# One pool of 4 KB tiles and longer leads in a two-layer decoder kernel

## The chip, the cores and the metric

The kernel runs on one core of a Trainium2 chip. The metric is the time of one execution on the device in microseconds; the time given for a kernel is the median of its runs.

## The reference

Two decoder layers on 512 rows of width 1024 in float32, each followed by a SwiGLU feed-forward with a hidden width of 2816. The first mixes by a gated MLP, the second by retention with four heads. Every part starts with an RMS norm, and the result is added to the stream.

```python
h = h + sgu_mixer(rmsnorm(h), ...)      # z = gelu(h @ w_in); u, v halves; u * (W_s LN(v) + b) @ w_out
h = h + swiglu(rmsnorm(h), ...)         # (silu(h @ w_g) * (h @ w_u)) @ w_down
h = h + retention(rmsnorm(h), ...)      # q, k rotated; decayed scores; group norm; * silu(g); @ w_out
h = h + swiglu(rmsnorm(h), ...)
return rmsnorm(h)
```

## The kernel before

All large products are made in float32 precision from three matmuls: each operand is split into a high part (fp32r) and a low part, and `three` adds high x high, high x low and low x high in PSUM. The high part of a weight tile is written by ACT and the low part by VectorE (DVE) in `split`; tiles of weights are 128 x 2 x 512, 4 KB per partition.

Blocks of 1024 x 512 pairs of columns use `seven`, a form of Strassen's product with the seven products P1, P7, P6, Q4, P5, P2, P3 in this order, on quarters of both operands: a gate-up unit (`gu`, five per feed-forward), a down product (`dn`, two per feed-forward, the rest goes through `last_rows`), values and gates of a head (`vg`, four) and half of the output projection of retention (`ro0`). Each of the seven has two jobs, one for each pair of row tiles. Sums of weight quarters come from VectorE, or, for P7 and P5 of `dn`, `vg` and `ro`, from an accumulating load that GpSimd's queue (POOL) issues after the plain load. Sums of the left factor's quarters are made on VectorE by the function `A` and split as well (`h_P7h`, `h_P7l` for instance); `run` asks for the left factors of its own product and of the next two.

The work is a list of jobs, and `pipeline` goes through it: before a job runs, weights are fetched up to six weighted jobs ahead (`FETCH`) and split up to three ahead (`PREP`). A scheduler then sets each engine's order of instructions when the program is built, by the order in which they were written and by when they could run, and tiles are given out of pools in which a new tile waits for an old one to be free. Pool `gen` has 21 tiles of 4 KB, `raws` 8 of 8 KB (rows of hidden values, left factors of the feed-forward and of the heads, copies of the normed input); `XH` and `XL`, the normed input's two parts, have a place of their own. SyncE's queue (SP) issues the plain loads.

The rotary tables (sine and cosine of position angles, some 36 VectorE instructions on 128 x 512) are made in eight steps during the first feed-forward, one after its small first unit (`gl`) and one or two in each unit after it.

Of the kernel before, what the change touches and what calls it, by code (L numbers as in the profile page):

```python
# [25 lines left out]
PREP = 3  # L26
FETCH = 6
N_GEN = 21
N_RAW = 8
N_TMP = 5  # L30
EPS = 1e-6
# [18 lines left out]
class Job:  # L50


    def __init__(self, fetch=None, prep=None, run=None):
        self.fetch, self.prep, self.run = fetch, prep, run


def pipeline(jobs):
    n = len(jobs)
    weighted = [i for i, j in enumerate(jobs) if j.prep is not None]
    f = p = 0  # L60
    done = 0
    for i, job in enumerate(jobs):
        while f < len(weighted) and f < done + FETCH:
            jobs[weighted[f]].fetch()
            f += 1
        while p < len(weighted) and p < done + PREP:
            jobs[weighted[p]].prep()
            p += 1
        if job.prep is not None:
            done += 1  # L70
        job.run()
# [3 lines left out]
def trunk(ctx, tc, x, positions, mix_g, ffn_g, fin_g, sgu_w_in, sgu_w_s, sgu_b_s, sgu_ln_g, sgu_ln_b,  # L75
# [5 lines left out]
    raws = ctx.enter_context(tc.tile_pool(name="raws", bufs=N_RAW))  # L81
# [10 lines left out]
    def RAW(name, dtype=F32, shape=(P, 4, T)):  # L92
        return raws.tile(list(shape), dtype, tag="r", name=name)
# [11 lines left out]

    def captured(*fns):

        n = len(jobs)
        for fn in fns:
            fn()  # L110
        new = jobs[n:]
        del jobs[n:]
        units = []
        for j in new:
            if j.prep is not None or not units:
                units.append([j])
            else:
                units[-1].append(j)
        return units

    def merged(a, b):

        i = j = 0
        while i < len(a) or j < len(b):
            if j == len(b) or (i < len(a) and i * len(b) <= j * len(a)):
                jobs.extend(a[i])
                i += 1
            else:
                jobs.extend(b[j])
                j += 1  # L130
# [82 lines left out]
    XH = xpool.tile([P, KD, T], F32R, name="XH")  # L213
    XL = xpool.tile([P, KD, T], F32R, name="XL")
    X = xpool.tile([P, NC, D], F32, name="X")

    def project_t(name, w, slices, evac, col_of=None, halves=False, mid=None):
# [4 lines left out]
        def run(kp, t0, t1):  # L222
            if not ps:
                ps.extend(PS(f"ps_{name}_{i}") for i in range(2))
            for m in range(4):
                o = ps[m // 2][:, m % 2, t0:t1]
                for a in range(2):
                    k = 2 * kp + a
                    sl = slice(m * P, (m + 1) * P)
                    first = k == 0 and (t1 == T)  # L230
                    three(o, ws[kp].h[:, a, sl], ws[kp].l[:, a, sl], XH[:, k, t0:t1], XL[:, k, t0:t1],
                          first, k == KD - 1)
# [32 lines left out]
    def natural_step(o, c, kp, w):  # L265
        wh, wl = w
        for a in range(2):
            k = 2 * kp + a
            sl = slice(c * P, (c + 1) * P)
            three(o, XH[:, k, sl], XL[:, k, sl], wh[:, a, :], wl[:, a, :], k == 0, k == KD - 1)  # L270
# [3 lines left out]

    def seven(name, w, r0, np_, c1, c2, A, evac, mid=None, dma_sums=False, turned=False):

# [3 lines left out]
        steps = [(s, min(2, np_ - s)) for s in range(0, np_, 2)]  # L280
# [4 lines left out]
        def load(key, i, j, s, nk):  # L285
            raw[key, s] = fetch_tile(f"{name}_{key}_{s}", w, r0 + i * np_ + s, nk, ((c1, T) if j == 0 else (c2, T),))

        def onto(key, i, j, s, nk):
            c0 = c1 if j == 0 else c2
            k0 = r0 + i * np_ + s  # L290
            src = w[k0 * P:(k0 + nk) * P, c0:c0 + T].rearrange("(a p) n -> p a n", p=P)
            nc.gpsimd.dma_start(raw[key, s][:, 0:nk, :], src, accum_op=ALU.add)

        def fetch(p, s, nk):
            if p == "P1":
                load("b11", 0, 0, s, nk)
            elif p == "P7" and dma_sums:
                load("t", 1, 1, s, nk)
                onto("t", 0, 1, s, nk)
            elif p == "P5" and dma_sums:  # L300
                load("b12", 0, 1, s, nk)
                onto("b12", 0, 0, s, nk)
            elif p == "P7":
                load("b12", 0, 1, s, nk)
                load("t", 1, 1, s, nk)
            elif p == "Q4":
                load("b21", 1, 0, s, nk)
            elif p == "P2":
                load("b21", 1, 0, s, nk)
            elif p == "P3":  # L310
                load("b22", 1, 1, s, nk)

        def add(dst, other, s, nk):
            d, o = raw[dst, s][:, 0:nk, :], raw[other, s][:, 0:nk, :]
            nc.vector.tensor_tensor(d, d, o, ALU.add)  # L315

        def prep(p, s, nk):
# [4 lines left out]
            parts[p, s] = split(raw[use, s], f"{name}_{p}_{s}", nk)  # L322

        chain = {"P1": "X", "P7": "Y", "P6": "X", "Q4": "Y", "P5": "X", "P2": "Z", "P3": "X"}
# [3 lines left out]
        def matmuls(p, s, nk, c):  # L328
            o = acc[chain[p]]
            ah, al = A(p)  # L330
            wh, wl = parts[p, s]
            cs = slice(c * P, (c + 1) * P)
            first, last = p in opens, p in closes
            if not turned:
                for a in range(nk):
                    k = s + a
# [790 lines left out]
```

## Time and profile before

| what | us |
|---|---|
| median of 3 runs | 1269.76 |
| lowest, highest run | 1268.45, 1273.49 |
| the profiled execution | 1267.79 |
| its span, first to last instruction | 1266.1 |

| engine | busy us | share |
|---|---|---|
| PE (TensorE matmul) | 1220.4 | 96% |
| PEld (TensorE weight load) | 1081.8 | 85% |
| DVE (VectorE) | 947.4 | 75% |
| ACT (ScalarE) | 616.8 | 49% |
| POOL (GpSimd) | 47.4 | 4% |

The profile names an instruction by its source line, engine, operation and tiles (`out<-in`, with the buffer numbers left out). Matmuls are pipelined and their ends are modelled, so PE idle is what no modelled matmul covers. A granted clock below 1.00 means that TensorE ran slower for a part of the stretch. A wait is put down to the operation that came last; "waited for: us in total, times, longest" stands at the end of such a row.

### The profile page before, as it was taken

What the parts mean: (1) busy time and instruction counts of PE and PEld (TensorE: products, weight loads), DVE (VectorE), ACT (ScalarE), POOL (GpSimd) and SP (SyncE); (2) the same over time, 40 slices, a digit from 0 to 9 for tenths busy, and PEclk for the clock granted to TensorE, in tenths of its full rate; (3) what the DMA queues carried; (4) which work ended last, traced back from release to release, by engine and by line L of the source; (5) the groups of instructions that cost most, each with busy time, mean ns of one, the idle gap of its engine ahead of it and who ended that gap; (6) DMA issues with size and microseconds to landing.
All of it is one profiled execution on the core that took longest, in us unless ns stands there. A gap on an engine that the chain in (4) does not pass through costs nothing. (4 is left out here: it accounts for less than half of the span.)

```text
span 1266.1 us, 18063 instructions
## 1 busy us (share of the span) xinstructions
PE 1220.4 (96%) x7290; PEld 1081.8 (85%) x7290; DVE 947.4 (75%) x1080; ACT 616.8 (49%) x772; POOL 47.4 (4%) x49
## 2 busy tenths in 40 slices
PE   8999999998999999999999999889999999999997
PEld 7787889987999798978878878668899989997995
DVE  4467489999779884786766757697488799878864
ACT  4424255544544463656455564465355445544452
POOL 0000000000001000000000000000000010000000
PEclk9999999999999999999999999899999999999999
DMA  7224225457636763356445645466215476556531
GB/s 266 85 83 128 64 84 156 137 146 228 183 117 164 219 198 94 84 156 169 127 140 125 185 123 150 110 178 211 84 44 174 142 175 196 170 158 187 189 116 67
DMA packets 101987, 183.91 MB, mean 145 GB/s; under 512 B 6376, under 2 KB 19728, under 8 KB 101904
## 3 DMA queue, kind: packets, MB, share of 16 engines
q1 hardware_dynamic: 91984, 163.86, 40.8%
q0 software_dynamic: 9920, 18.90, 9.1%
q8 instruction: 57, 0.93, 0.3%
q14 instruction: 26, 0.21, 0.1%
HBM read 180.64 MB, written 2.10 MB: 144 GB/s over the span
## 5 line engine op out<-in xcount | busy, mean ns | idle before, releaser
L211 PE MATMUL X_gu<-xP_f,wl_gu_P 128*128 128x256 f32 x480 | 135.8, 283 | 0.0
L210 PE MATMUL X_gu<-xP_f,wh_gu_P 128*128 128x256 f32 x480 | 135.8, 283 | 0.0
L209 PE MATMUL X_gu<-xP_f,wh_gu_P 128*128 128x256 f32 x480 | 135.8, 283 | 0.0
L188 DVE TENSOR_TENSOR wl_gu_P<-wr_gu_b,wh_gu_P 128x1024 fp32r<-128x1024 f32 x80 | 95.0, 1219 | 29.6 <-ACT wh_gu_P L187 29.6
L210 PEld LDWEIGHTS X_gu<-xP_f,wh_gu_P 128*128 128x128 f32 x480 | 92.1, 192 | 0.2
L209 PEld LDWEIGHTS X_gu<-xP_f,wh_gu_P 128*128 128x128 f32 x480 | 92.1, 192 | 0.2
L211 PEld LDWEIGHTS X_gu<-xP_f,wl_gu_P 128*128 128x128 f32 x480 | 92.1, 192 | 0.0
L187 ACT ACTIVATE wh_gu_P<-wr_gu_b 128x1024 fp32r<-128x1024 f32 x80 | 79.5, 1052 | 18.4 <-DVE wl_gu_P L188 5.0
L315 DVE TENSOR_TENSOR wr_gu_t<-wr_gu_t,wr_gu_b 128x1024 f32<-128x1024 f32 x60 | 71.7, 1217 | 2.1 <-DMA wr_gu_t<-in_ffn_w_gu 2.0
L187 ACT ACTIVATE wh_gu_P<-wr_gu_t 128x1024 fp32r<-128x1024 f32 x40 | 41.6, 1057 | 50.3 <-DVE wr_gu_t L315 40.6
L188 DVE TENSOR_TENSOR wl_vg_P<-wr_vg_b,wh_vg_P 128x1024 fp32r<-128x1024 f32 x32 | 38.6, 1219 | 26.8 <-ACT wh_vg_P L187 26.8
L209 PE MATMUL ps_qk<-XH,wh_qk 128*128 128x512 f32 (+1 forms) x160 | 56.1, 352 | 1.4 <-ACT xr_r L622 0.8
L211 PE MATMUL ps_qk<-XH,wl_qk 128*128 128x512 f32 (+1 forms) x160 | 55.6, 348 | 0.0
L210 PE MATMUL ps_qk<-XL,wh_qk 128*128 128x512 f32 (+1 forms) x160 | 55.4, 347 | 0.0
L188 DVE TENSOR_TENSOR wl_gu_P<-wr_gu_t,wh_gu_P 128x1024 fp32r<-128x1024 f32 x40 | 48.0, 1218 | 7.1 <-ACT wh_gu_P L187 7.1
L209 PE MATMUL Y_gu<-xP_f,wh_gu_P 128*128 128x256 f32 x160 | 45.3, 283 | 0.0
L210 PE MATMUL Y_gu<-xP_f,wh_gu_P 128*128 128x256 f32 x160 | 45.3, 283 | 0.0
L211 PE MATMUL Y_gu<-xP_f,wl_gu_P 128*128 128x256 f32 x160 | 45.3, 283 | 0.0
L209 PE MATMUL Y_gu<-XH,wh_gu_Q 128*128 128x256 f32 x160 | 45.3, 283 | 0.0
L210 PE MATMUL Y_gu<-XL,wh_gu_Q 128*128 128x256 f32 x160 | 45.3, 283 | 0.0
L211 PE MATMUL Y_gu<-XH,wl_gu_Q 128*128 128x256 f32 x160 | 45.3, 283 | 0.0
L209 PE MATMUL Z_gu<-XH,wh_gu_P 128*128 128x256 f32 x160 | 45.3, 283 | 0.0
(507 smaller groups left out, 3872.9 us busy)
## 6 DMA issues: line engine op xcount, KB each, us to landing
wr_gu_b<-in_ffn_w_gu SPq DMA_DIRECT2D x100, 512.0 KB, 4.0
wr_dn_b<-in_ffn_w_down SPq DMA_DIRECT2D x40, 512.0 KB, 4.6
wr_vg_b<-in_ret_w_in SPq DMA_DIRECT2D x40, 512.0 KB, 3.7
wr_gu_t<-in_ffn_w_gu SPq DMA_DIRECT2D x20, 512.0 KB, 5.2
wr_qk<-in_ret_w_in SPq DMA_DIRECT2D x32, 256.0 KB, 3.1
wr_dn<-in_ffn_w_down SPq DMA_DIRECT2D x12, 512.0 KB, 4.0
wr_ro_b<-in_ret_w_out SPq DMA_DIRECT2D x10, 512.0 KB, 4.1
wr_u<-in_sgu_w_in SPq DMA_DIRECT2D x8, 512.0 KB, 4.1
```

Of the source, the lines that this page charges most:

```text
L187: nc.scalar.activation(h, s, AF.Copy)
L188: nc.vector.tensor_tensor(l, s, f32(h), ALU.subtract)
L209: nc.tensor.matmul(o, ah, bh, start=start, stop=False, skip_group_check=True)
L210: nc.tensor.matmul(o, ah, bl, start=False, stop=False, skip_group_check=True)
L211: nc.tensor.matmul(o, al, bh, start=False, stop=stop, skip_group_check=True)
L315: nc.vector.tensor_tensor(d, d, o, ALU.add)
```

## The change

It has five parts. All 4 KB work goes into one pool `gen` of 38 tiles: 8 KB tiles are cut into a tile for each half of the rows or for each of the high and low parts, and `raws` is gone (`XH` and `XL` get a pool of two tiles). Weights are split five jobs ahead instead of three and fetched eight ahead instead of six, and the accumulating loads with their base loads twelve ahead (`EARLY`). `seven` takes groups of rows (one group in each use here), and in the gate-up units P5 loads both its quarters anew instead of keeping P1's and P7's: 40 more loads of 512 KB. The left factors P1, P7 and P6 of a product are asked for in the block before it, where it was P1 and P7, or P1 alone. The rotary tables' eight steps go to the eight jobs of `u0` and `u1` in the mixing layer.

```diff
-PREP = 3
-FETCH = 6
-N_GEN = 21
-N_RAW = 8
+PREP = 5
+FETCH = 8
+EARLY = 12
+ASK = 3
+N_GEN = 38
+SUMS_X = ("P7", "P5")
+SUMS_GU = ()
...
-    for i, job in enumerate(jobs):
-        while f < len(weighted) and f < done + FETCH:
-            jobs[weighted[f]].fetch()
+    for job in jobs:
+        while e < n and e < done + EARLY:
+            if weighted[e].early:
+                weighted[e].fetch()
+            e += 1
+        while f < n and f < done + FETCH:
+            if not weighted[f].early:
+                weighted[f].fetch()
             f += 1
...
-    raws = ctx.enter_context(tc.tile_pool(name="raws", bufs=N_RAW))
+    xp = ctx.enter_context(tc.tile_pool(name="xp", bufs=2))
...
+            if p == "P7":
+                load("t", 1, 1)
+                (onto if p in dma_sums else load)("t" if p in dma_sums else "o", 0, 1)
...
+            elif p == "P5":
+                load("b12", 0, 1)
+                (onto if p in dma_sums else load)("b12" if p in dma_sums else "o", 0, 0)
...
-            extra = {"P7": "b12", "P6": "b11", "Q4": "b21", "P5": "b11"}.get(p)
-            if extra and not (dma_sums and p in ("P7", "P5")):
-                add(use, extra, s, nk)
+            extra = {"P7": "o", "P6": "b11", "Q4": "b21", "P5": "o"}.get(p)
+            if extra and p not in dma_sums:
...
-                h, l = RAW(f"{name}_h{r}", F32R), RAW(f"{name}_l{r}", F32R)
-                for a in range(0, n, 2):
+                h, l = (G(f"{name}_{q}{r}_{i}", F32R, (P, 4, H))[:, 0:len(ks), :] for q in "hl")
...
+    project_t("u0", w_in, ((0, T),), after_u0, mix0_col, mid={kp: turn_tables for kp in range(4)})
+    project_t("u1", w_in, ((T, T),), after_u1, mix0_col, mid={kp: turn_tables for kp in range(4)})
...
-            nc.vector.tensor_tensor(yraw[j][:, i, :], u, mx[g // 2][:, g % 2, :], ALU.mult)
+            for h in range(2):
+                hs = slice(h * H, (h + 1) * H)
+                nc.vector.tensor_tensor(yq[j][h][:, i, :], u[:, hs], mx[g // 2][:, g % 2, hs], ALU.mult)
...
-        unit(1, {"P5": lambda: A[0]("P1"), "P2": lambda: A[0]("P7")})
+        unit(1, {("Q4", 1): lambda: A[0]("P1", 0), ("P5", 0): lambda: A[0]("P7", 0), ("P2", 1): lambda: A[0]("P6", 0)})
         down(0)
...
-        second({"P2": lambda: outA("P1")} if hd == 3 else None)
+        second({("P6", 1): lambda: outA("P1", 0), ("P2", 0): lambda: outA("P7", 0), ("P2", 1): lambda: outA("P6", 0)} if hd == 3 else None)
```

VectorE's order around the start of the output projection of retention. `vg3` is the last head, `y7_3<-X_vg3` the evacuation of its P5, `s1_3<-Z_vg3` that of its P2, `z...` are left factors, `wl_ro0_...` low parts of the projection's weights, and `X_97<-X_97,X_ro0` adds its first product. Before:

```order
L1016 TENSOR_TENSOR y7_3_6898<-y7_3_6898,X_vg3_6819 128x1024
L992 TENSOR_TENSOR s3_3_7069<-sc3_2_7052,dec3_6809 128x128
L188 TENSOR_TENSOR wl_vg3_P3_0_7076<-wr_vg3_b22_0_6965,wh_vg3_P3_0_7075 128x1024
L995 TENSOR_TENSOR sl3_6990<-s3_3_7069,sh3_6988 128x128
L188 TENSOR_TENSOR wl_vg3_P3_2_7096<-wr_vg3_b22_2_7013,wh_vg3_P3_2_7095 128x1024
L1010 TENSOR_TENSOR s1_3_6850<-s1_3_6850,Z_vg3_7079 128x1024
L1013 TENSOR_TENSOR vl3_0_7113<-s1_3_6850,vh3_0_7112 128x1024
L415 TENSOR_TENSOR z0_P1l_7117<-z0_5564,z0_P1h_7116 128x1024
L188 TENSOR_TENSOR wl_ro0_P1_0_7124<-wr_ro0_b11_0_7031,wh_ro0_P1_0_7123 128x1024
L188 TENSOR_TENSOR wl_ro0_P1_2_7128<-wr_ro0_b11_2_7073,wh_ro0_P1_2_7127 128x1024
L188 TENSOR_TENSOR wl_ro0_P7_0_7159<-wr_ro0_t_0_7092,wh_ro0_P7_0_7158 128x1024
L388 TENSOR_TENSOR z0_S3_7163<-z0_5564 128x1024
```

After:

```order
L1008 TENSOR_TENSOR y7_3_6999<-y7_3_6999,X_vg3_6924 128x1024
L984 TENSOR_TENSOR s3_1_7117<-sc3_0_7100,dec3_6914 128x384
L984 TENSOR_TENSOR s3_2_7165<-sc3_2_7158,dec3_6914 128x256
L170 TENSOR_TENSOR wl_ro0_P1_0_0_7180<-wr_ro0_b11_0_0_7073,wh_ro0_P1_0_0_7179 128x1024
L370 TENSOR_TENSOR z_S3_0_7196<-z0_0_5677,z0_1_5663 128x1024
L987 TENSOR_TENSOR sl3_7098<-s3_1_7117,sh3_7096 128x384
L1002 TENSOR_TENSOR s1_3_6954<-s1_3_6954,Z_vg3_7183 128x1024
L987 TENSOR_TENSOR sl2_3_7099<-s3_2_7165,sh2_3_7097 128x256
L397 TENSOR_TENSOR z_P7l_0_7199<-z_S3_0_7196,z_P7h_0_7198 128x1024
L984 TENSOR_TENSOR s3_3_7175<-sc3_2_7158,dec3_6914 128x128
L170 TENSOR_TENSOR wl_ro0_P1_0_2_7206<-wr_ro0_b11_0_2_7121,wh_ro0_P1_0_2_7205 128x1024
L1005 TENSOR_TENSOR vl3_0_7223<-s1_3_6954,vh3_0_7222 128x1024
```

The first cast of the projection moved ahead of the evacuation `s1_3<-Z_vg3`, and P1's factor (further up) and P7's stand before the projection's first product.

VectorE's order in the first down product of the first feed-forward (`dn0_0`). `quarter_turns` is the last of the rotary tables, `X_97` (after: `X_95`) with `X_dn0_0` is the addition of P1, `wr_dn0_0_t_...` a sum of weights. Before:

```order
L388 TENSOR_TENSOR h0_0_S1_2515<-h0_0_1638,h0_1_2099 128x1024
L840 TENSOR_TENSOR quarter_turns_3458<-quarter_3456,turn19_3459 128x512
L315 TENSOR_TENSOR wr_dn0_0_t_0_2410<-wr_dn0_0_t_0_2410,wr_dn0_0_b11_0_2332 128x1024
L388 TENSOR_TENSOR h0_0_S2_2517<-h0_0_S1_2515,h0_0_1638 128x1024
L415 TENSOR_TENSOR h0_0_P6l_2520<-h0_0_S2_2517,h0_0_P6h_2519 128x1024
L188 TENSOR_TENSOR wl_dn0_0_P7_2_2538<-wr_dn0_0_t_2_2449,wh_dn0_0_P7_2_2537 128x1024
L918 SCALAR_TENSOR_TENSOR h0_1_2099<-X_gu0_1_2043,s1_0_1_2100 128x2x256
L428 TENSOR_TENSOR X_97<-X_97,X_dn0_0_2514 128x2x512
L188 TENSOR_TENSOR wl_dn0_0_P6_0_2558<-wr_dn0_0_t_0_2410,wh_dn0_0_P6_0_2557 128x1024
```

After:

```order
L370 TENSOR_TENSOR h0_0_S2_0_2537<-h0_0_S1_0_2535,h0_0_0_1818 128x1024
L397 TENSOR_TENSOR h0_0_P6l_0_2540<-h0_0_S2_0_2537,h0_0_P6h_0_2539 128x1024
L170 TENSOR_TENSOR wl_dn0_0_P7_0_0_2547<-wr_dn0_0_t_0_0_2302,wh_dn0_0_P7_0_0_2546 128x1024
L410 TENSOR_TENSOR X_95<-X_95,X_dn0_0_2613 128x2x512
L170 TENSOR_TENSOR wl_dn0_0_P7_0_2_2553<-wr_dn0_0_t_0_2_2338,wh_dn0_0_P7_0_2_2552 128x1024
L891 SCALAR_TENSOR_TENSOR h0_1_0_2269<-X_gu0_1_2142,s1_0_1_2200 128x512
L302 TENSOR_TENSOR wr_dn0_0_t_0_0_2302<-wr_dn0_0_t_0_0_2302,wr_dn0_0_b11_0_0_2371 128x1024
L302 TENSOR_TENSOR wr_dn0_0_t_0_2_2338<-wr_dn0_0_t_0_2_2338,wr_dn0_0_b11_0_2_2407 128x1024
L170 TENSOR_TENSOR wl_dn0_0_P6_0_0_2610<-wr_dn0_0_t_0_0_2302,wh_dn0_0_P6_0_0_2609 128x1024
L410 TENSOR_TENSOR X_95<-X_95,Y_dn0_0_2649 128x2x512
```

The rotary row is gone; the addition of P1 moved ahead of P7's second cast, and the sum of weights for P6 that stood ahead of it stands behind it. P6's factor stands ahead of that addition in both.

VectorE's order in the mixing layer, between the statistics of `v` (`mv`, and the steps `ri_ln`, `ry_ln`, `rt_ln` of its inverse root) and its normalization; `wl_u1_...` are casts for the second half of `u`, `sum`, `turn`, `turns` and `frac` rotary steps. Before:

```order
L528 SCALAR_TENSOR_TENSOR ry_ln_0_554<-ru_ln_0_552,ry_ln_548 128x4
L192 SCALAR_TENSOR_TENSOR wl_u1_1_680<-wr_u1_1_509,mix0_cols_108,wh_u1_1_679 128x512
L524 TENSOR_TENSOR rt_ln_1_556<-ry_ln_0_554 128x4
L526 SCALAR_TENSOR_TENSOR ru_ln_1_558<-rt_ln_1_556,ra_ln_544 128x4
L528 SCALAR_TENSOR_TENSOR ry_ln_1_560<-ru_ln_1_558,ry_ln_0_554 128x4
L524 TENSOR_TENSOR rt_ln_2_562<-ry_ln_1_560 128x4
```

After:

```order
L518 SCALAR_TENSOR_TENSOR ry_ln_0_570<-ru_ln_0_568,ry_ln_564 128x4
L734 CAST turn6_728<-sum5_726 128x512
L742 TENSOR_SCALAR turns7_761<-ahl_645 128x512
L514 TENSOR_TENSOR rt_ln_1_572<-ry_ln_0_570 128x4
L735 TENSOR_TENSOR turns_686<-sum5_726,turn6_728 128x512
L734 CAST turn8_764<-turns7_761 128x512
L516 SCALAR_TENSOR_TENSOR ru_ln_1_574<-rt_ln_1_572,ra_ln_560 128x4
L735 TENSOR_TENSOR frac7_763<-turns7_761,turn8_764 128x512
L518 SCALAR_TENSOR_TENSOR ry_ln_1_576<-ru_ln_1_574,ry_ln_0_570 128x4
L757 TENSOR_TENSOR sum8_767<-turns_686,frac7_763 128x512
L514 TENSOR_TENSOR rt_ln_2_578<-ry_ln_1_576 128x4
```

Where single casts stood between the steps of the inverse root, one to three table steps stand now between one and the next; on those steps the normalization of `v` waits.

More of the change, by code (lines that the diff above doesn't have):

```diff
@@ L104, in trunk @@
     jobs = []
[L106 to L130, printed above, removed]
     def then(fn):
@@ L294, in fetch @@
[L294 to L305, printed above, removed]
+            return w[k0 * P:(k0 + nk) * P, c0:c0 + T].rearrange("(a p) n -> p a n", p=P)
@@ L375, in combos @@
-    def combos(name, raw, np_):
+                    matmuls(p, g, s, nk, c)
+            elif n == len(steps) - 1:
+                for c in range(2):
+                    for st_ in steps[-2:]:
+                        matmuls(p, *st_, c)
+                    evac(p, acc, c)
+            if mid and (p, n) in mid:
+                mid[p, n]()
+        for i in range(len(PRODUCTS) * len(steps)):
+            p, st_ = PRODUCTS[i // len(steps)], steps[i % len(steps)]
+            jobs.append(Job(lambda p=p, st_=st_: fetch(p, *st_), lambda p=p, st_=st_: prep(p, *st_), lambda i=i: run(i),
+                            early=p in dma_sums))
@@ L492, in chunk, with start @@
                     step(kp, j, c)
+        def start(kp, j):
+            left(where[2 * kp][0], 1)
+            step(kp, j, 3)
+            left(where[2 * kp][0], 0)
         ends = list(range(n_all, kt // 2))
@@ L874, in feed_forward @@
+    def feed_forward(l, ready):
         w = ffn_w_gu[l]
-        hraw = [None] * 5
-        hlast = []
+        hq = [[None, None] for _ in range(5)]
+        he = []
         xparts = xA(f"f{l}")
-        steps = iter(range(100))
-        def more():
-            if extra is not None:
-                extra(next(steps))
         def first_evac(ps):
```

446 lines of the change are left out of this document (221 added, 225 removed).

## The prediction

> **What bounds the kernel now.** I read the page's first part and its totals, then the busy time by stretches of the program, then what TensorE waited for, then the order of time around the worst waits. The page's first rows:
>
> ```profile
> PE 1220.4 (96%) x7290; PEld 1081.8 (85%) x7290; DVE 947.4 (75%) x1080; ACT 616.8 (49%) x772; POOL 47.4 (4%) x49
> HBM read 180.64 MB, written 2.10 MB: 144 GB/s over the span
> ```
>
> TensorE is busy 1220.4 of 1266.1 us, and the change leaves it the same matmuls, so only its idle time and its slow clock can be won. The next rows cut the span at the stages (stretch, width, PE busy and its instructions, granted clock, DMA share and rate); the difference of the first two numbers is idle.
>
> ```profile
> 0.00:45.00 45.00, 38.58 (x171) 1.00 0.65 222
> 45.00:165.00 120.00, 118.56 (x563) 1.00 0.32 99
> 165.00:185.00 20.00, 17.51 (x148) 1.00 0.01 4
> 185.00:262.00 77.00, 77.00 (x644) 1.00 0.48 144
> 262.00:310.00 48.00, 44.01 (x220) 0.96 0.73 195
> 395.00:430.00 35.00, 33.07 (x153) 1.00 0.70 188
> 505.00:600.00 95.00, 92.15 (x516) 1.00 0.52 134
> 600.00:803.00 203.00, 198.97 (x913) 1.00 0.54 142
> 803.00:860.00 57.00, 48.50 (x194) 0.91 0.59 159
> 905.00:945.00 40.00, 37.62 (x286) 1.00 0.26 80
> 1030.00:1060.00 30.00, 29.35 (x130) 1.00 0.88 261
> 1130.00:1185.00 55.00, 52.35 (x280) 1.00 0.72 198
> 1240.00:1266.10 26.10, 17.75 (x77) 0.95 0.22 81
> ```
>
> Idle is 6.4 us in the start, 1.4 in the mixing layer, 2.5 and 2.4 where a feed-forward begins, 4.0, 1.9, 0.7 and 2.7 in the four down products (the first is 262 to 310), 6.9 in the retention heads (505 to 803), 8.5 in the output projection of retention (803 to 860), 8.4 at the end. The gate-up stage 185 to 262 has none. Who is waited for:
>
> ```profile
> PE ps_gl L210 <- DVE XL L592: 5.2, 4, 2.5
> PE X_ro L209 <- ACT wh_ro_P L187: 4.4, 2, 2.7
> PE Y_dn L209 <- ACT wh_dn_Q L187: 3.2, 4, 2.6
> PE Z_vg L210 <- DVE wl_vg_P L188: 2.0, 3, 1.0
> PE pv L209 <- ACT vh L1012: 1.6, 2, 0.8
> ```
>
> All are operands that ACT and VectorE split from raw tiles. The order of time shows one such wait and what follows it:
>
> ```profile
> 285.69 0.39 PE L209 MATMUL X_dn<-wh_dn_P,h_P6h 128*128 128x512 f32 x1
> 288.68 0.47 PE L209 MATMUL Y_dn<-wh_dn_Q,h_Q4h 128*128 128x512 f32 x1 [2.61 <-ACT wh_dn_Q L187]
> 289.73 0.50 PE L210 MATMUL X_dn<-wl_dn_P,h_P6h 128*128 128x512 f32 x1 [0.57 <-DVE wl_dn_P L188]
> ...
> 401.13 0.39 PE L210 MATMUL Y_dn<-wl_dn_P,h_P7h 128*128 128x512 f32 x1
> 401.36 0.39 PE L211 MATMUL Y_dn<-wh_dn_P,h_P7l 128*128 128x512 f32 x1
> 401.58 0.28 PE L209 MATMUL X_gu<-xP_f,wh_gu_P 128*128 128x256 f32 x1
> 401.70 0.28 PE L210 MATMUL X_gu<-xP_f,wh_gu_P 128*128 128x256 f32 x1
> ...
> 808.34 0.80 PE L210 MATMUL X_ro<-wl_ro_P,z_P1h 128*128 128x512 f32 x1 [0.84 <-DVE wl_ro_P L188]
> 808.93 0.63 PE L211 MATMUL X_ro<-wh_ro_P,z_P1l 128*128 128x512 f32 x1
> 809.36 0.63 PE L209 MATMUL X_ro<-wh_ro_P,z_P1h 128*128 128x512 f32 x1
> ```
>
> A matmul of 512 columns follows the last after 0.23 us (401.13 to 401.36), one of 256 after 0.12 (401.58 to 401.70). The wait listed at 2.61 costs 2.99 - 0.23 = 2.76, so each listed wait hides some 0.2 us under the modelled end of the matmul before it, and shorter ones hide wholly. After the waits at 803 to 808 matmuls start 0.43 us apart (808.93 to 809.36): the clock is halved, as the 0.91 of that stretch and the 0.96 of 262 to 310 say. Lost clock there is 0.09 x 57 + 0.04 x 48 = 7.1 us, idle matmul time included; of it I count 4.6, some 23 matmuls at 0.2.
>
> The Trainium skill, TensorE: Matmul & The Clock Gate, Part 1, says the clock drops to half after an idle window of about 3.4 us and comes back after as much work. The trace agrees in kind: 2.61 + 0.57 us of idle is followed by a drop, the 2.5 at 165 to 185 by none. By that rule three drops cost 1.7 us each, 5.1 instead of my 4.6, and all go once no gap nears the window.
>
> **Why VectorE is late there.** Its instructions follow each other every 1.13 us:
>
> ```profile
> 282.78 1.22 DVE L315 TENSOR_TENSOR wr_dn_t<-wr_dn_t,wr_dn_b 128x1024 f32<-128x1024 f32 x1
> 283.92 1.22 DVE L388 TENSOR_TENSOR h_S<-h_S,h 128x1024 f32<-128x1024 f32 x1
> ...
> L839 DVE CAST turn<-sum x5: 416/421/427, 207.8 to 259.6; 128x512 int32<-128x512 f32 x5
> L840 DVE TENSOR_TENSOR turns<-sum,turn x5: 679/682/684, 211.0 to 263.3; 128x512 f32<-128x512 f32 x5
> ...
> 45.00:110.00 65.00, 65.00 (x301) 53.72 (x300) 34.77 (x70) 17.29 (x26) 1.09 (x1) 1.00 0.27 82
> 245.00:285.00 40.00, 39.19 (x275) 36.65 (x274) 38.56 (x42) 21.24 (x23) 2.60 (x3) 1.00 0.60 163
> ```
>
> A down product has 14 low parts of weights, 4 sums of weights, 7 low parts and 4 sums of left factors and 7 additions into X: 36 x 1.13 = 40.7 us, against 168 matmuls x 0.227 = 38.1 on TensorE. A gate-up unit has 14 + 8 on weights and 4 whole and 2 half evacuations, 26 x 1.13 + 2 x 0.6 = 30.6, against 336 x 0.12 = 40.3. So the products lack 2.6 us and the units have 9.7 to spare; only work done ahead can close it. In the first pair the rotary tables lie on top: VectorE is busy 38.56 of 40 us in 245 to 285 (third pair of numbers of the row), though only 34.77 of 65 in the mixing layer.
>
> **The change, part by part.**
>
> *Left factors a unit ahead.* P6 (two sums, one low part, 3.4 us) joins P1 and P7 in the unit before: unit 37.4 of 40.3, product 34 of 38.1. Both fit now. Not all is covered: after the change X's first addition still waits for the first product and a queue stands behind it: 16 instructions up to the cast of Q4's second part (the order rows show the first of them), 14 x 1.13 + 2 x 0.6 = 17 us, and TensorE reaches that part about as much later (P7 and P6, half of Q4 and half of the unit's last product: 60 x 0.227 + 24 x 0.12 = 16.5). I leave 1.3 us at each down product (between 0 and the 2.7 of the row 1130 to 1185).
>
> *Parts five jobs ahead instead of three.* A job is 2.7 us in a down product, so a cast gains up to 5.4 us of lead where VectorE has time. In the projection of retention that is what lacks: in the order before, its first cast stands behind the evacuation of the head's last product; after, three instructions behind `y7_3`, with P7's and P6's factors ahead of the first addition into X. The stage now costs 8.5 idle + 3.2 of the 4.6 for the clock + some 7 waits x 0.2 hidden = 13.1; I leave 2.3, since the last head's output still runs through VectorE there. Where a feed-forward begins, the four waits on `XL` (5.2 us by the row, 6 with their hidden parts) come from casts and rotary work queued between the transposes' evacuations; with the casts done earlier I leave 1.2 of them. What is late next there is the norm of the last rows, which nothing moves.
>
> *Accumulating loads twelve ahead.* ACT waits for them in the heads:
>
> ```profile
> ACT wh_vg_P L187 <- DMA wr_vg_b<-in_ret_w_in: 16.2, 4, 5.5
> wr_vg_b<-in_ret_w_in POOLq DMA_DIRECT2D x8, 512.0 KB, 7.4
> wr_gu_b<-in_ffn_w_gu SPq DMA_DIRECT2D x100, 512.0 KB, 4.0
> 1040.00:1060.00 20.00, 19.35 (x85) 15.38 (x85) 18.03 (x17) 11.95 (x12) 0.00 (x0) 1.00 0.93 288
> ```
>
> A load of 4.0 us and an accumulation of 7.4 follow each other, 11.4 us, and the lead of six jobs was 6 x 2.7 = 16, with a tile to wait for first; twelve are 33. P5's base load now goes out before Q4's. The heads cost 6.9 + some 9 waits x 0.2 = 8.7; the waits on Z and on late parts go, the one for the last evacuation (`pv`, up to 0.8 at each of four heads) stays: 3.2 left.
>
> *Forty more loads.* P5 fetches its second part again instead of keeping it: 40 x 0.52 MB = 21 MB beside 180.6 read. A gate-up unit goes from 12 loads to 16, 8.4 MB in 40.3 us, 208 GB/s. The quoted stretch moved 288, so transfers stay hidden: 0 us on the path, at worst a landing of 4.0 us late once per unit if SP's queue runs behind. P5's sum is one VectorE instruction as before.
>
> *Rotary tables in the mixing layer.* Some 36 instructions of 128x512 at 0.42 to 0.68, about 20 us, come out of 140 to 275 and go where VectorE has 30 to spare. But between the last `v` and `u0` they share the queue with the normalization of `v`, which TensorE needs for the mixing matmuls: the order rows show table steps between the steps of its inverse root. From the last statistics of `v` to its last normalization stand 49 instructions, about 21 us of VectorE work by these durations, and the matmuls of `u0` from there are 84 x 0.227 = 19. I add 1.6 us (between 0 and the 20 if nothing hid them). The 8 extra half evacuations of `y` and 2 of the small unit, 0.3 to 0.7 us each, lie beside matmuls; their cover gone they would cost 3 to 7.
>
> **The sum**, in us: projection of retention 13.1 to 2.3, -10.8; first down product 4.0 + 1.4 clock + 0.5 hidden = 5.9 to 1.3, -4.6; the other three 5.3 + 1.3 hidden to 3.9, -2.7; feed-forward starts -4.8; heads -5.5; mixing +1.6; start and end 0. That is -26.8, and -2 for waits too short to be listed: -29. The profiled execution took 1267.8 (span 1266.1 and 1.7 around it), 0.15% below the median of 1269.8; from the median, 1241.
>
> **Rivals.** *VectorE stays the bound.* Lead does not help an engine with no time: then only the rotary share (-3.5 in the first product), the retention projection's earlier factors (-7), the feed-forward starts (-4) and +1.6 remain, -13: 1257. For it: 40.7 against 38.1 us. For it too: in the order rows P6's factor still stands just ahead of the product's first addition. Against: the units' slack, and the rotary row that is gone.
>
> *Tiles run out, slower.* One pool of 38 tiles holds six jobs' parts (12), about 10 raw tiles, 8 left factors, 4 of hidden rows, 3 evacuations and the small unit's 2: 39. A cast or load that waits for a tile would give one wait like that at 288.68 in each block of seven products, 2.8 + 0.4 + 1.4 clock = 4.6 us; over 19 blocks 87, less 29: 1328. It decides from 6 blocks on. Against: loads wait for matmuls now (SP's waits) without idle in 185 to 262, and the order puts casts and loads earlier everywhere I looked. The Trainium skill, Perfetto Trace Analysis, Optimization Strategy, says that a gap repeating on the engine that should be saturated can mean SBUF is short for the next tile; no run here shows it yet.
>
> *The lead isn't taken,* since the order is fixed when the program is built: 1268. The order rows speak against it.
>
> *All waits go:* also what I leave, 4 x 1.3 + 2.3 + 3.2 + 1.2 = 12: 1229.
>
> **How the numbers follow.** The forecast gets 0.64, VectorE as bound 0.20, all waits gone 0.05, no lead 0.05, tiles 0.06. The forecast's own bounds are 1233 (half of the 12 left goes too, and mixing costs nothing) to 1253 (the 12 are twice that); with the two rivals beside it 8 in 10 need 1228 to 1259. 0.5% (6.3 us) is about what a measurement of this kernel can tell from no change: faster is 0.64 + 0.20 + 0.05 = 0.89, within it 0.05, slower 0.06.
>
> **What would show it.** Right: in the profile after, PE idle under 3 us in the retention projection and under 1.5 in each down product, granted clock 1.00 in both, no `turn` rows after 130 us, ACT's wait for `wr_vg_b` under 3 us, DMA read near 201.6 MB. Wrong: the same names waited for in the down products with VectorE over 95% (first rival), or new waits in gate-up stretches that have none now (second).

## The result and the profile after

The kernel after takes 1232.93 us (median of 4 runs, 1232.21 to 1233.65) against 1269.92 before (median of 4): a ratio of 0.9705, with a 95% interval from 0.9684 to 0.9726. The forecast was 1241 in a range of 1228 to 1259. The profiled executions took 1267.79 before and 1233.38 after, 34.4 us less; the medians differ by 37.0 us, and the rest of that is spread between runs.

The page of after, the same two rows as of before:

```profile
PE 1208.4 (98%) x7290; PEld 1079.0 (88%) x7290; DVE 946.9 (77%) x1092; ACT 608.5 (49%) x772; POOL 47.4 (4%) x49
HBM read 201.61 MB, written 2.10 MB: 165 GB/s over the span
```

TensorE runs the same 7290 instructions, and VectorE is as busy as before (946.9 us, 947.4 before). 21 MB more are read. The busy time by stretches, cut at the same stages (width, PE busy and its instructions, granted clock, DMA share and rate):

```profile
184.00:261.00 77.00, 77.00 (x644) 1.00 0.69 211
261.00:304.00 43.00, 42.37 (x222) 1.00 0.70 208
389.00:422.00 33.00, 32.37 (x153) 1.00 0.69 215
589.00:786.00 197.00, 197.00 (x911) 1.00 0.52 142
786.00:831.00 45.00, 43.40 (x194) 1.00 0.70 205
1000.00:1027.00 27.00, 26.37 (x132) 1.00 0.74 246
1098.00:1149.00 51.00, 50.37 (x282) 1.00 0.71 207
```

The four down products (261, 389, 1000, 1098) are idle for 0.63 us each, the heads from the second on (589 to 786) not at all, the output projection of retention (786) for 1.6 us where it was 8.5, and the clock is 1.00 in every one. The gate-up stretch (184) has no idle time, as before. What TensorE still waits for, with the us in total, the times and the longest:

```profile
PE mix_ps L150 <- DMA mix_rows<-in_mix_norm_g: 2.9, 1, 2.9
PE Y_dn L193 <- DVE h_Q4l L397: 2.5, 4, 0.6
PE ps_gl L192 <- DVE XL_f L584: 1.7, 4, 0.6
PE Y_ro L191 <- ACT wh_ro_P L169: 1.6, 1, 1.6
```

The first is in the program's start, before any part of the change. Of the others only `h_Q4l` comes back at every down product. The other signs given for a right forecast hold as well: the last `turn` row starts at 110.1 us, and ACT no longer waits for `wr_vg_b` (16.2 us before).

**Lost time by stage.** Below, a stage's lost time is the distance of each matmul's start from the one before it, less 0.227 us (512 columns), 0.172 (384), 0.120 (256) or 0.109 (128), added over the stage. This counts idle time, its part hidden under a modelled end, and the slow clock together. The stages are cut at the same counts of matmuls in every kernel. The feed-forward column holds gate-up units and down products, the projection column the whole output projection of retention; the heads column begins with the norm ahead of the retention layer.

| kernel | us | start | mixing | feed-forward starts | feed-forwards | heads | projection | all |
|---|---|---|---|---|---|---|---|---|
| before | 1269.9 | 11.3 | 4.1 | 5.8 | 15.4 | 11.2 | 14.9 | 64.1 |
| after | 1232.9 | 12.1 | 4.4 | 2.0 | 5.2 | 2.6 | 2.1 | 29.7 |
| leads of before | 1290.2 | 11.8 | 5.2 | 2.0 | 38.5 | 16.0 | 10.8 | 85.5 |
| parts 3 ahead | 1274.6 | 11.7 | 5.2 | 2.0 | 27.2 | 15.4 | 8.4 | 71.0 |
| parts 4 ahead | 1255.8 | 10.9 | 5.2 | 2.0 | 17.4 | 8.7 | 8.6 | 53.9 |
| parts 6 ahead | 1241.7 | 12.2 | 4.3 | 2.0 | 13.7 | 3.1 | 0.2 | 36.6 |
| loads 6 ahead | 1276.8 | 12.4 | 4.3 | 1.1 | 36.6 | 6.6 | 7.2 | 69.2 |
| accumulating loads 8 ahead | 1238.5 | 11.3 | 4.3 | 2.0 | 5.5 | 3.0 | 3.4 | 30.7 |
| left factors as before | 1254.2 | 11.2 | 4.4 | 2.0 | 18.6 | 3.1 | 10.7 | 51.1 |
| rotary as before | 1239.2 | 11.4 | 3.4 | 2.1 | 10.1 | 2.6 | 4.1 | 34.7 |
| 34 tiles | 1235.7 | 12.3 | 4.4 | 2.0 | 5.2 | 5.0 | 2.1 | 32.1 |
| P5's parts kept | 1233.2 | 12.2 | 4.3 | 2.0 | 5.1 | 2.6 | 2.0 | 29.3 |
| Q4's factor ahead too | 1231.5 | 14.0 | 4.3 | 2.0 | 2.1 | 2.6 | 2.0 | 28.4 |
| before, longer lead | 1291.8 | 11.6 | 14.9 | 12.8 | 16.9 | 16.6 | 14.1 | 88.3 |

The last column (the end of the program, 1.1 to 1.3 us, is in it) fell by 34.4 us from before to after, which is all of the difference of the profiled times. The table is from one profiled execution of each kernel, so differences of 1 us in it, and those of the start, which varies from 10.9 to 14.0 us, say little. The question for the experiments is which part of the change did it.

### The profile page after: what moved, and what is told of

Its sections match the earlier page's. It is cut to its first block, busy times and chain, and to the rows that moved or that the text cites. A ratio compares the mean times of both kernels' runs of the same rounds, so it can differ in the third digit from the quotient of the medians.

```text
span 1231.7 us, 18116 instructions
## 1 busy us (share of the span) xinstructions
PE 1208.4 (98%) x7290; PEld 1079.0 (88%) x7290; DVE 946.9 (77%) x1092; ACT 608.5 (49%) x772; POOL 47.4 (4%) x49
## 4 chain that ended last, share of the span: by engine, by line
PE 86%; DVE 9%; ACT 3%; issue 2%; DMA 0%; SPq 0%; DVEq 0%; ACTq 0%
PE X_gu L193 6%; PE X_gu L192 6%; PE X_gu L191 6%; PE Y_gu L193 3%; PE Y_gu L192 3%; PE Y_gu L191 3%; PE X_vg L191 2%; PE X_vg L193 2%; PE X_vg L192 2%; PE ps_qk L192 2%; PE ps_qk L193 2%; PE ps_qk L191 2%; PE X_dn L191 2%; PE X_dn L192 2%; PE X_dn L193 2%
## 5 line engine op out<-in xcount | busy, mean ns | idle before, releaser
L169 ACT ACTIVATE wh_gu_P<-wr_gu_t 128x1024 fp32r<-128x1024 f32 x40 | 42.4, 1059 | 59.4 <-DVE wr_gu_t L302 58.2
L192 PE MATMUL ps_qk<-XL_r,wh_qk 128*128 128x512 f32 (+1 forms) x160 | 55.7, 348 | 0.6 <-DVE XL_r L584 0.6
L191 PE MATMUL ps_qk<-XH_r,wh_qk 128*128 128x512 f32 (+1 forms) x160 | 55.5, 349 | 0.0
L193 PE MATMUL ps_qk<-XH_r,wl_qk 128*128 128x512 f32 (+1 forms) x160 | 55.2, 348 | 0.0
L191 PE MATMUL Y_gu<-xP7h_f,wh_gu_P 128*128 128x256 f32 x160 | 45.3, 283 | 0.0
L192 PE MATMUL Y_gu<-xP7l_f,wh_gu_P 128*128 128x256 f32 x160 | 45.3, 283 | 0.0
L193 PE MATMUL Y_gu<-xP7h_f,wl_gu_P 128*128 128x256 f32 x160 | 45.3, 283 | 0.0
L191 PE MATMUL X_gu<-xP6h_f,wh_gu_P 128*128 128x256 f32 x160 | 45.3, 283 | 0.0
L192 PE MATMUL X_gu<-xP6l_f,wh_gu_P 128*128 128x256 f32 x160 | 45.3, 283 | 0.0
L193 PE MATMUL X_gu<-xP6h_f,wl_gu_P 128*128 128x256 f32 x160 | 45.3, 283 | 0.0
L191 PE MATMUL Y_gu<-XH_f,wh_gu_Q 128*128 128x256 f32 x160 | 45.3, 283 | 0.0
```

The lines of the kernel that those rows point to most:

```text
L169: nc.scalar.activation(h, s, AF.Copy)
L191: nc.tensor.matmul(o, ah, bh, start=start, stop=False, skip_group_check=True)
L192: nc.tensor.matmul(o, ah, bl, start=False, stop=False, skip_group_check=True)
L193: nc.tensor.matmul(o, al, bh, start=False, stop=stop, skip_group_check=True)
```

## Experiments

### The leads set back

```diff
-PREP = 5
-FETCH = 8
-EARLY = 12
+PREP = 3
+FETCH = 6
+EARLY = 6
```

> The kernel after, with parts three jobs ahead, loads six ahead and accumulating loads six ahead, as before; everything else as after. Theory 1 (the longer lead carries the gain outside the first down product and the left factors): the heads give back most of their 8.6 us, the starts of the feed-forwards 3, the retention projection 5, the other down products 2: about 1251 us. Theory 2 (the one pool and the earlier left factors carry it, since VectorE cannot be more than three jobs ahead anyway): within 4 us of after, 1233 to 1237.

It took 1290.22 us, 1.0155 of before (1.0123 to 1.0187): slower than before, which neither theory had. Without the longer leads the other parts of the change cost 20 us. The feed-forwards lose 38.5 us where before lost 15.4. The runs that follow take the leads apart.

### Parts three jobs ahead, loads as after

```diff
-PREP = 5
+PREP = 3
```

> The kernel after with parts split three jobs ahead instead of five; loads stay eight and twelve ahead. The run with all three leads cut took 1290. Theory 1 (what was lost there is VectorE's time ahead): most of it again, 1265 to 1290, with the waits in the heads and the down products for parts, not for loads. Theory 2 (it was the loads: an accumulating load that was asked for six jobs ahead lands late): 1233 to 1245.

1274.55 us, 1.0022 of before (1.0005 to 1.0038): theory 1, to the middle of its range. Each down product now begins with a late part, and behind its two waits matmuls start 0.43 us apart (272.26 to 272.69), which is the halved clock. The timeline of this run around the first one, TensorE and then ACT and VectorE:

```profile
270.22 0.80 PE L191 MATMUL X_dn<-wh_dn_P,h_P1h 128*128 128x512 f32 x1 [2.79 <-ACT wh_dn_P L169]
271.67 0.80 PE L192 MATMUL X_dn<-wl_dn_P,h_P1h 128*128 128x512 f32 x1 [0.65 <-DVE wl_dn_P L170]
272.26 0.63 PE L193 MATMUL X_dn<-wh_dn_P,h_P1l 128*128 128x512 f32 x1
272.69 0.63 PE L191 MATMUL X_dn<-wh_dn_P,h_P1h 128*128 128x512 f32 x1
...
266.97 1.06 ACT L904 ACTIVATE s<-s 128x1024 f32<-128x1024 f32 x1 [6.39 <-DVE s L903]
268.17 1.06 ACT L396 ACTIVATE h_P6h<-h_S 128x1024 fp32r<-128x1024 f32 x1
269.13 1.99 ACT L169 ACTIVATE wh_dn_P<-wr_dn_b 128x1024 fp32r<-128x1024 f32 x2
...
269.25 1.22 DVE L397 TENSOR_TENSOR h_P6l<-h_S,h_P6h 128x1024 fp32r<-128x1024 f32 x1 [1.18 <-ACT h_P6h L396]
270.39 2.35 DVE L170 TENSOR_TENSOR wl_dn_P<-wr_dn_b,wh_dn_P 128x1024 fp32r<-128x1024 f32 x2
```

P6's left factor, which the change asks for in the unit, stands on both engines ahead of the casts of P1's weights: `h_P6h` at 268.17 ahead of `wh_dn_P` at 269.13, `h_P6l` at 269.25 ahead of `wl_dn_P` at 270.39. TensorE needs the casts first and P6's factor two products later. That is the smaller part of the 2.79 us: the factor holds ACT for 0.96 us. The larger part stands before it. ACT was idle for 6.39 us until the unit's evacuation `s` could run at 266.97, and with three jobs of lead the casts stand behind it. The same casts in after, with five jobs of lead, stand 8 to 11 us earlier, ahead of `s` (there at 266.56) and of P6's factor (`h_P6l` at 268.85):

```profile
258.18 1.99 ACT L169 ACTIVATE wh_dn_P<-wr_dn_b 128x1024 fp32r<-128x1024 f32 x2
261.91 2.35 DVE L170 TENSOR_TENSOR wl_dn_P<-wr_dn_b,wh_dn_P 128x1024 fp32r<-128x1024 f32 x2
```

So the lead has to carry the casts past the unit's last evacuation, and by this timeline the factors a unit ahead make a late cast about 1 us later. No run has the parts three ahead with the left factors as before, so that cost is read off here and not measured.

### Four and six jobs

```diff
-PREP = 5
+PREP = 4
```

> The kernel after with parts four jobs ahead; three gave 1274.6, five 1232.9. Theory 1 (each job of lead is 2.7 us and the waits fall evenly): about 1250. Theory 2 (there is a threshold, the longest stretch in which VectorE and ACT are held by a wait in their order): near one of the two, 1235 or 1270.

1255.84 us, 0.9878 (0.9854 to 0.9901): theory 1. The time falls by about as much with each job, 1274.6, 1255.8 and 1232.9 us for three, four and five.

```diff
-PREP = 5
-FETCH = 8
+PREP = 6
+FETCH = 9
```

> The kernel after with parts six and loads nine jobs ahead, in the same 38 tiles. Theory 1 (VectorE's slack in the units is not used up): 1229 to 1232. Theory 2 (tiles: two more for parts out of 38, where 34 cost 0 to 3 us): 1235 to 1250, with the losses at the layers' starts, where the longer lead in the old pools lost most.

1241.69 us, 0.9766 (0.9744 to 0.9788), so slower than after and in theory 2's range; but the reason of theory 2 is wrong. The layers' starts did not move (feed-forward starts 2.0 in both), and the projection won 1.9 us. The loss is in the down products. The timeline in the first of them, VectorE and then TensorE:

```profile
285.52 1.22 DVE L170 TENSOR_TENSOR wl_dn_Q<-wr_dn_t,wh_dn_Q 128x1024 fp32r<-128x1024 f32 x1
286.65 1.21 DVE L410 TENSOR_TENSOR X<-X,X_dn 128x1024 f32<-128x1024 f32 x1
287.79 1.22 DVE L397 TENSOR_TENSOR h_Q4l<-h,h_Q4h 128x1024 fp32r<-128x1024 f32 x1
...
289.06 0.50 PE L193 MATMUL Y_dn<-wh_dn_Q,h_Q4l 128*128 128x512 f32 x1 [2.25 <-DVE h_Q4l L397]
```

The same place in after:

```profile
285.25 1.22 DVE L170 TENSOR_TENSOR wl_dn_Q<-wr_dn_t,wh_dn_Q 128x1024 fp32r<-128x1024 f32 x1
286.38 1.22 DVE L397 TENSOR_TENSOR h_Q4l<-h,h_Q4h 128x1024 fp32r<-128x1024 f32 x1
...
287.65 0.50 PE L193 MATMUL Y_dn<-wh_dn_Q,h_Q4l 128*128 128x512 f32 x1 [0.63 <-DVE h_Q4l L397]
```

In after, Q4's low part stands behind the first of Q4's two casts and ahead of the second and of the addition into X; with six jobs it stands behind both casts (the first at 281.16) and the addition. Four waits of 0.6 become four of 2.25, and two of these are followed by the halved clock (last section). A cast done too early is in the way too, though this one costs 9 us where one job too few costs 23. The Trainium skill, Perfetto Trace Analysis, Tensor Engine Instruction, says that ACT and VectorE take their instructions strictly in the order of their queue. These two timelines agree: Q4's low part comes when the rows ahead of it are done, at 287.79 and at 286.38.

### Loads six jobs ahead

```diff
-FETCH = 8
-EARLY = 12
+FETCH = 6
+EARLY = 6
```

> The kernel after with all loads, the accumulating ones too, six jobs ahead; parts stay five ahead. Theory 1 (the parts' lead decides): 1233 to 1245. Theory 2 (loads that land late decide; a base load and its accumulation take 11 us and have five jobs less lead to land in before the part is asked for): 1265 or more, and ACT waits for wr_vg_b and wr_dn_b by over 20 us.

1276.83 us, 1.0044 (1.0022 to 1.0066): theory 2, and not for the accumulating loads alone. Among this run's waits:

```profile
PE Y_dn L192 <- DVE wl_dn_P L170: 8.3, 4, 2.1
ACT wh_dn_P L169 <- DMA wr_dn_b<-in_ffn_w_down: 27.7, 8, 5.7
ACT wh_gu_P L169 <- DVE wr_gu_t L302: 81.6, 22, 11.2
```

With parts five ahead a load that is six ahead has one job, about 2.7 us, to land before its split. By the page of after (KB of one load, us to landing) that is too short:

```profile
wr_gu_b<-in_ffn_w_gu SPq DMA_DIRECT2D x100, 512.0 KB, 3.8
wr_gu_o<-in_ffn_w_gu SPq DMA_DIRECT2D x40, 512.0 KB, 4.7
```

ACT waits for it, and behind ACT the low parts, up to 2.1 us at each down product. (The third row alone would not show it: ACT waits 58.2 us for `wr_gu_t` in after too.) In after the loads run three jobs ahead of the parts.

This run, the two with parts three ahead and after make a table of four. With both leads short the ratio to before is 1.0155; with the longer lead of the loads alone 1.0022, with that of the parts alone 1.0044, with both 0.9705. Each alone wins a little over 1%, both together 4.5%.

### Accumulating loads eight ahead instead of twelve

```diff
-EARLY = 12
+EARLY = 8
```

> The kernel after with the accumulating loads and their base loads eight jobs ahead, like all other loads, instead of twelve. Theory 1 (the term of the heads: a base load and its accumulation take 11 us and twelve jobs cover that with a tile to wait for): the heads, the projection and the down products lose 0.5 to 2 us each, 1238 to 1250. Theory 2 (eight jobs of 2.7 us, less the five of the parts' lead, are 8 us and nearly cover it): 1233 to 1236.

1238.48 us, 0.9746 (0.9719 to 0.9773): at the lower edge of theory 1, but its interval overlaps that of after. The runs lie between 1234.41 and 1240.80, and the profiled one is the lowest, so its trace (lost time 30.7 us, 1.0 more than after) does not show what the others lost. In that trace the heads lose 3.0 us, where after loses 2.6 and before 11.2, and ACT waits for accumulated parts again, as it does not in after, but with little of it reaching TensorE:

```profile
ACT wh_dn_P L169 <- DMA wr_dn_b<-in_ffn_w_down: 9.2, 4, 2.7
ACT wh_vg_P L169 <- DMA wr_vg_t<-in_ret_w_in: 2.0, 1, 2.0
```

The medians differ by 5.6 us and the profiled executions by 1.0; how much the twelve jobs bring beyond eight, and where, stays open.

### The left factors as before

```diff
-    unit(1, {("Q4", 1): lambda: A[0]("P1", 0), ("P5", 0): lambda: A[0]("P7", 0), ("P2", 1): lambda: A[0]("P6", 0)})
+    unit(1, {("P5", 1): lambda: A[0]("P1", 0), ("P2", 1): lambda: A[0]("P7", 0)})
...
-    unit(4, {("P2", i): lambda i=i: lefts[f"dn{l}_2"](0, 1 - i) for i in range(2)})
+    unit(4)
...
-    second({("P6", 1): lambda: outA("P1", 0), ("P2", 0): lambda: outA("P7", 0), ("P2", 1): lambda: outA("P6", 0)} if hd == 3 else None)
+    second({("P2", 1): lambda: outA("P1", 0)} if hd == 3 else None)
```

The second down product is changed in the same way, and the last rows of the projection, whose left factors the change also asks for earlier.

> The kernel after, with the left factors asked for as before (P1 after P5 and P7 after P2 in a unit, P1 alone after P2 of the last head; none ahead for the last rows). Theory 1 (left factors ahead carry the down products and half of the projection): down products back by 6 us, projection by 6: about 1245. Theory 2 (the order put P6's factor at the product's start in both, so the lead of the casts does the work): up to 2 us slower in all, 1233 to 1235.

1254.18 us, 0.9871 (0.9849 to 0.9894): theory 1, and more than it asked. The down products lose 4.1 us each (after 1.2), 11 of the 21; of the 4.1 the wait is some 2.2 and the halved clock behind it 1.7. In the first, P6's low part is made inside the product, behind the additions into X:

```profile
280.10 1.21 DVE L410 TENSOR_TENSOR X<-X,Y_dn 128x1024 f32<-128x1024 f32 x1
281.23 1.22 DVE L397 TENSOR_TENSOR h_P6l<-h_S,h_P6h 128x1024 fp32r<-128x1024 f32 x1
...
282.50 0.50 PE L193 MATMUL X_dn<-wh_dn_P,h_P6l 128*128 128x512 f32 x1 [2.00 <-DVE h_P6l L397]
```

The projection's seven products do not lose (2.0 in both); its last rows do, 8.6 us, of which one wait of 5.4 is for the left part `ro_h`. So P7's and P6's factors in the last head bring nothing there; the factors of the last rows do. But before lost only 0.2 us in these rows without asking ahead: the factors of the last rows make good a wait that the other parts of the change bring with them.

```profile
PE ps_ro L191 <- ACT ro_h L445: 5.4, 1, 5.4
```

### Rotary tables back in the first feed-forward

The eight steps stand after the small first unit, P6 and P5 of the gate-up units, as before, instead of in `u0` and `u1`.

> The kernel after, with the rotary tables back in the first feed-forward, in the same eight steps as before. Theory 1 (the rotary steps fill VectorE and make the first product late): the first down product loses 4 to 5 us and the mixing layer wins 0.3: about 1237. Theory 2 (with the longer lead the units' slack absorbs them): 1233, within 1.

1239.2 us, 0.976 (0.9744 to 0.9775): theory 1. Lost time goes up by 4.3 us in the first down product, 0.8 in the unit before it and 2.0 in the projection (from a change of order that I did not follow), and down by 1.0 in the mixing layer and 0.7 in the start. In the first product the row of this run (width, then PE, PEld, VectorE, ACT) has VectorE busy for 47.49 of 48 us:

```profile
260.00:308.00 48.00, 44.91 (x228) 37.99 (x227) 47.49 (x46) 25.94 (x28) 2.39 (x2) 0.96 0.66 200
```

### Fewer tiles, and P5's parts kept

```diff
-N_GEN = 38
+N_GEN = 34
```

> The kernel after with 34 tiles instead of 38 in the one pool. Theory 1 (tiles are the store that the lead lives on): loads and casts wait for tiles, and each of 19 blocks loses 1 to 4.6 us: 1250 to 1320. Theory 2 (the lead in time is set by VectorE's speed, and there are tiles to spare): within 2 us of after, 1231 to 1235.

1235.65 us, 0.9732 (0.9716 to 0.9747). Nearly theory 2, which ended at 1235. The interval overlaps that of after; the trace has 2.4 us more lost, all in the heads, and ACT's casts of weights wait longer for matmuls that they do not read (some 26 us in all, 6.6 in after). Four tiles are worth some 2 us by the trace, and not told apart from nothing by the time.

```diff
-                (onto if p in dma_sums else load)("t" if p in dma_sums else "o", 0, 1)
+                (onto if p in dma_sums else load)("t" if p in dma_sums else "b12", 0, 1)
...
-            elif p == "P5":
-                load("b12", 0, 1)
+            elif p == "P5" and p in dma_sums:
+                load("b12", 0, 1)
...
-            extra = {"P7": "o", "P6": "b11", "Q4": "b21", "P5": "o"}.get(p)
+            extra = {"P7": "b12", "P6": "b11", "Q4": "b21", "P5": "b11"}.get(p)
```

> The kernel after with the gate-up units' P5 made of the kept tiles again (no second load: 40 loads of 512 KB fewer, and two tiles per step held for longer). Theory 1 (the loads lie beside the matmuls and the tiles suffice, as the prediction has it): 1233, within 2 us. Theory 2 (loading anew frees tiles, four of 38 over half a unit, which the lead lives on): 1238 to 1260, with waits in the gate-up units and the down products. Theory 3 (the 21 MB more cost something): 1229 or less.

1233.16 us, 0.9696 (0.9666 to 0.9725), with 180.64 MB read: theory 1. The forty loads cost nothing and, with 38 tiles, bring nothing.

### The longer lead alone, in the kernel before

```diff
-PREP = 3
-FETCH = 6
+PREP = 5
+FETCH = 8
```

> The kernel before with parts five jobs and loads eight jobs ahead, in its own pools of 21 and 8 tiles. Theory 1 (the lead is what the change needs, the pools are only its form): the retention projection wins 8 to 12 and the heads 5: 1250 to 1258. Theory 2 (21 tiles of 4 KB hold no longer lead: ten for parts and ten for raw tiles leave one for everything else): casts and loads wait for tiles, 1265 to 1300.

1291.83 us, 1.0158 (1.0127 to 1.0189): theory 2. The waits of this run, and ACT's timeline at the start of the first feed-forward:

```profile
ACT wh_gu_P L187 <- PE ps_so L211: 16.8, 1, 16.8
ACT wh_gu_P L187 <- PE ps_ro L211: 16.8, 1, 16.8
PE xT_f L589 <- DVE xs_f L603: 7.7, 4, 2.2
...
156.62 1.06 ACT L187 ACTIVATE wh_gu_P<-wr_gu_b 128x1024 fp32r<-128x1024 f32 x1 [16.84 <-PE ps_so L211]
157.98 1.06 ACT L561 ACTIVATE sq_so<-X 128x1024 f32<-128x1024 f32 x1 [0.30 <-PE ps_so L211]
```

The cast at 156.62 needs nothing from the product `ps_so`; it waits 16.84 us for that product's last matmul. I found nothing that ties the two but the tile that the cast is to write, which the product must still be reading. The other runs bear this out: after has the same lead and 38 tiles and no such row, and with 34 tiles the two rows are back at 3.3 and 2.4 us. Behind it on ACT stands the square of the norm, `sq_so`, and behind that the normed rows `xs_f` that TensorE waits for. Mixing layer and feed-forward starts lose 17.8 us more than before. The heads column loses 5.4 more: 8.0 at the start of the retention layer, while the heads themselves win 2.5. The Trainium skill, Perfetto Trace Analysis, Optimization Strategy, says that a repeating gap on the engine that should be saturated can mean that SBUF is short for the next tile. This trace agrees, at the starts of the layers, and the sign of it is a releaser that the waiting instruction does not read from (16.8 us, twice).

### Q4's factor ahead too

```diff
-("P2", 1): lambda: A[0]("P6", 0)})
+("P2", 0): lambda: A[0]("P6", 0), ("P2", 1): lambda: A[0]("Q4", 0)})
```

> The kernel after with Q4's left factor, too, asked for in the unit before (P6's after P2's first half, Q4's after its second). Theory 1 (what is left at each down product is VectorE's queue behind the first addition, of which Q4's low part is the last row): 0.9 of the 1.25 us goes at each of four, 1229. Theory 2 (two more tiles and two more instructions in the unit, which has 2.9 us of slack): 1233 or up to 4 us more.

1231.48 us, 0.9684 (0.9663 to 0.9706). The second down product is changed in the same way. The four waits for `h_Q4l` are gone: the first of its rows starts at 271.8, where it was 286.4.

```profile
L397 DVE TENSOR_TENSOR h_Q4l<-h,h_Q4h x4: 1217/1218/1220, 271.8 to 1110.3; 128x1024 fp32r<-128x1024 f32 x4
```

The feed-forwards lose 2.1 us instead of 5.2, as theory 1 has it, but the median is only 1.5 us below after's and the intervals overlap; the profiled run has 1.9 us more in the start, which the edit does not touch. It is the fastest kernel here, and not told apart from after by its time.

## Why the prediction was right, and where not

**The time** came out 8 us below the forecast, inside the range and at the lower bound, 1233, that the forecast had without its rivals. Term by term, in lost time of the two profiles: the projection fell by 12.8 (forecast 10.8), the first down product by 5.2 (4.6), the other three from 8.5 to 3.8, by 4.7 (2.7), the feed-forward starts by 3.8 (4.8), the heads by 8.6 (5.5); mixing rose by 0.3 (1.6), the start by 0.8 (0). The 2 us set aside for waits too short to be listed were too few: the sum had 8.7 us in the heads and 6.6 in the three products, where 11.2 and 8.5 were lost before. Its 4.6 us for the halved clock were too few as well: the three drops at 290, 808 and 846 us cost 1.7, 1.9 and 1.8 by the starts of the matmuls, 5.4. The mixing term was right in kind: with the tables back in the feed-forward the mixing layer loses 1.0 less (1.6 in the sum), and 0.7 less than in before. The 1.3 left at each down product was measured at 1.2 to 1.3, and its place is the one in the sum: VectorE's queue behind the first addition into X. The sum counted to the cast of Q4's second part; what TensorE waits for is Q4's left factor, two instructions ahead of that cast.

**The step that was too pessimistic** was the heads: I left 3.2 us for the evacuation `pv` waits for, and it went with the rest. Taking half of the gain for the accumulating loads' lead was the wrong cause: with these eight jobs ahead the heads lose 3.0 in the profiled run, and with parts three ahead and the loads as in after 15.4. With parts five ahead and all loads six they lose 6.6. It is the parts' lead that the heads lived on first of all.

**VectorE's slack.** The forecast has a product of 34 us of VectorE work beside 38.1 of matmuls, and the sign I gave for the first rival was VectorE over 95% busy in a down product with the same names waited for. In the stretch that the table has of the second product VectorE is over 95% busy:

```profile
389.00:422.00 33.00, 32.37 (x153) 26.74 (x152) 31.61 (x29) 17.54 (x18) 0.00 (x0) 1.00 0.69 215
```

It is 31.61 of 33 us there, with 0.6 us of waiting, and 35.4 of 38 us, 93%, over the whole product (386 to 424). In before it was 44.57 of 48 in the first product (262 to 310), 93% too, with TensorE idle for 4.0 us. VectorE goes on to later casts when it is done: at 421.11 it is at one of the next unit (`wl_gu_P`). So the busy share could not tell the rival from the forecast; the names waited for did.

**What the parts are worth.** The sum gave each part of the change a gain of its own. The runs show that most of the gain comes only when the parts stand together. The lead alone, in the old pools, costs about 20 us (ratio 1.0158), by the very mechanism of the second rival, which I had looked for only in the new pool. The rest with all leads short costs 20 us too, and either lead on top of it alone only leads back to the time of before (1.0022 and 1.0044). The left factors asked for earlier, those of the last rows with them, are worth 21 us with the lead, of which 8.6 are in the last rows, where before had no such loss; what they cost without the lead is not measured. In the projection the cause was only half right: P7's and P6's factors in the last head do nothing, the casts' lead does. So the total came out closer than its causes, and that is in part luck. That new loads cost nothing, and that the rotary move is worth about what the first product lost, held.

**The rivals.** VectorE as the bound would have given 1257, all waits gone 1229; the result lies nearer the second. Neither a pool of 38 tiles nor one of 34 runs out in the rival's sense. SP's loads do wait for matmuls (128.8 us for `X_gu` in after, 111.1 before), but hardly any of it reaches TensorE.

## What to carry to other kernels

A lead is a chain: tiles to hold it, loads further ahead than splits, splits further ahead than the operands that are asked for in the same queues; set one link alone and most of the gain stays away, and where tiles are short it turns into a loss. Try the neighbours of a lead on both sides, since on an engine that works in order a cast that is too early delays the operand needed next, as a late cast does. When an instruction waits for an engine whose result it does not read, look for a tile that is not free.

## What was not expected of the hardware

How long TensorE waits does not by itself say whether the clock halves behind the wait. In the run with parts three ahead, in the values of the first head, two short waits are enough:

```profile
553.34 0.49 PE L191 MATMUL X_vg<-wh_vg_P,xP6h_r 128*128 128x512 f32 x1 [0.52 <-ACT wh_vg_P L169]
555.85 0.50 PE L192 MATMUL X_vg<-wl_vg_P,xP6h_r 128*128 128x512 f32 x1 [2.02 <-DVE wl_vg_P L170]
...
556.53 0.63 PE L191 MATMUL X_vg<-wh_vg_P,xP6h_r 128*128 128x512 f32 x1
556.96 0.63 PE L192 MATMUL X_vg<-wl_vg_P,xP6h_r 128*128 128x512 f32 x1
```

Idle of 0.52 and 2.02 us, one matmul apart, is followed by starts 0.43 us apart, seven of them, 1.4 us lost. A single wait can do it too: with the left factors as before each of the four waits of 2.00 us for `h_P6l` is followed by such starts. With parts six ahead one and the same wait, for `h_Q4l`, does both. In the first down product (the row at 289.06 above) the clock stays, in the second it halves:

```profile
289.39 0.39 PE L191 MATMUL Y_dn<-wh_dn_Q,h_Q4h 128*128 128x512 f32 x1
289.62 0.39 PE L192 MATMUL Y_dn<-wl_dn_Q,h_Q4h 128*128 128x512 f32 x1
...
410.38 0.50 PE L193 MATMUL Y_dn<-wh_dn_Q,h_Q4l 128*128 128x512 f32 x1 [2.25 <-DVE h_Q4l L397]
...
411.67 0.63 PE L192 MATMUL Y_dn<-wl_dn_Q,h_Q4h 128*128 128x512 f32 x1
412.10 0.63 PE L193 MATMUL Y_dn<-wh_dn_Q,h_Q4l 128*128 128x512 f32 x1
```

The third and fourth products repeat this, without and with a drop, and a drop costs 1.7 us there. The wait of 2.5 us at a feed-forward start of before was followed by none, and neither was the 1.6 in after's projection. The Trainium skill, TensorE: Matmul & The Clock Gate, Part 1, gives an idle window of about 3.4 us. The drops shown here came after 2.0 to 2.5 us of listed idle; what decides between a drop and none stays open.
